# A first end output in a load buffer, and two of the last outputs stored in uneven partition pieces, in a rotation of an 8192x8192 matrix

## The chip, the cores and the metric

The kernel runs on one core of one Trainium2 chip. The time is the device time of that core in microseconds (us), as the median of several executions; the profiled execution is one more look, with its own span.

## The reference

```
x: 8192 x 8192 float32, k = 1
out = np.rot90(x, 1)          # out[r, c] = x[c, 8191 - r]
```

Each of 268 MB is read once and written once; nothing is computed.

## The kernel before

The matrix goes through the core in blocks of up to 1024 rows by 4096 columns. A block is loaded 128 rows at a time (2 MB per load, SyncE queue), VectorE reverses the columns within each block of 128 into small `ar` tiles, PE transposes 128x128 blocks into PSUM, ScalarE copies 128x2048 results to an `o` tile and issues its store on its own queue (2 MB per store). The last block is cut in two of 512 rows, called here the last two tiles; each has four outputs of 2 MB, `i` = 0 to 3, and the very last one is stored in two halves by columns. There are three `o` buffers and two `a` (load) buffers; at the end, when loads have run out, some outputs go to `a` buffers.

```python
def store(r0, rt, c0, chunks, end):
    ...
    for i, g0 in enumerate(range(0, W // P, G)):       # G = 8 blocks of 128 columns here
        if end and i % 2:
            ot = a_pool.tile([P, F], dt, tag="a")       # 2 buffers
        else:
            ot = o_pool.tile([P, F], dt, tag="o")       # 3 buffers
        o = ot[:, : G * rows].rearrange("m (g f) -> m g f", g=G)
        ...                                             # PE transposes into ps
            nc.scalar.copy(o[:, G - PW - h : G - h, :], ps[h // PW])
            done = h + PW
            if done % S == 0:
                dst = out[top : top + S * P, r0 : r0 + rows].rearrange("(g m) f -> m g f", g=S)
                nc.scalar.dma_start(out=dst, in_=o[:, G - done : G - done + S, :])
        yield
...
*_, chunks = load(*before_last)
outputs = store(*before_last, chunks, True)
rows = load(*last)
for _ in range(last[1] - 1):     # three of the four last loads
    next(rows)
next(outputs)                    # first end output
chunks = next(rows)              # the fourth load
```

## Time and profile before

| | before |
|---|---|
| time, median of 6 runs | 1267.64 us (1267.44 to 1268.09) |
| span of the profiled run | 1265.4 us |
| moved by DMA, over the span | 537.55 MB, 425 GB/s |
| busy share of PE, ScalarE, VectorE | 57%, 37%, 28% |

It is read by elimination: no compute engine is busy for more than 57% of the span, while the DMA engines are busy in all 40 slices. The lines for this, and what follows from them, stand in the prediction. One view that is used all through this text is not a view of the page: the completion records. A whole store adds to its semaphore 16 times in the trace, as many as the core has DMA engines (the page counts 4144 packets under 512 B, 16 for each of 128 loads and 131 stores); each increment is read here as one engine's, and sorted they show how many engines are early or late. They don't name the engine. The prediction's list times the small packets that write these increments; the increments themselves, used from here on, come some 0.4 us later (1264.32 and 1264.37 for its 1263.9 and 1264.0). In the views PE is TensorE and PEld its weight loads, DVE is VectorE, ACT is ScalarE, ACTq is ScalarE's instruction queue, where the issue of a DMA shows as the time that it holds the queue, and L167 is a line of the kernel.

### The profile page before, as it was taken

Reading aid. Unit: us, or ns where it says so; the run is one execution under the profiler, and the core shown is the slowest. Engines: PE = TensorE matmul, PEld = TensorE weight load, DVE = VectorE, ACT = ScalarE, POOL = GpSimd, SP = SyncE. Lnnn points to the kernel's source line nnn. Section 1 sums busy time; section 2 is a strip of 40 time slices with the busy share of each in tenths; the row PEclk is TensorE's granted clock in tenths of the full one; section 3 lists DMA queues with packets and bytes.
Section 4 is the critical chain, followed back from the end, with each engine's and each line's share of the span. In section 5 each row is a group of like instructions: output and inputs, shape, how many; then the busy total and the mean of one; then the engine's idle time right before and its main releaser. Section 6 shows DMA issues by size and latency. Waiting matters only on the chain.

```text
span 1265.4 us, 10391 instructions
## 1 busy us (share of the span) xinstructions
PE 721.2 (57%) x4096; PEld 680.0 (54%) x4096; DVE 355.2 (28%) x1024; ACT 466.6 (37%) x257; POOL 0.7 (0%) x6
## 2 busy tenths in 40 slices
PE   1554555566555565565655666556555566566573
PEld 1453555566545565555645655456555555555573
DVE  4423223322232222322233222322233222332210
ACT  0432433433334333343334333343333433343354
POOL 0000000000000000000000000000000000000000
PEclk9977777767777768777687776866867867767787
DMA  9999999999999999999999999999999999999998
GB/s 398 428 428 430 427 428 429 429 431 428 428 429 427 430 429 430 428 430 429 428 428 430 429 430 428 428 430 428 429 430 428 429 427 430 426 428 427 428 380 355
DMA packets 37345, 537.55 MB, mean 425 GB/s; under 512 B 4144, under 2 KB 4144, under 8 KB 4144
## 3 DMA queue, kind: packets, MB, share of 16 engines
q10 hardware_dynamic: 18864, 268.44, 50.0%
q1 hardware_dynamic: 18432, 268.44, 49.7%
q8 instruction: 32, 0.52, 0.2%
q14 instruction: 17, 0.14, 0.0%
HBM read 268.44 MB, written 268.44 MB: 424 GB/s over the span
## 4 chain that ended last, share of the span: by engine, by line
DMA 84%; ACT 13%; issue 1%; PE 0%; ACTq 0%; DVE 0%; SPq 0%
DMA out_dram<-ot 81%; ACT ot L167 13%; DMA a<-in_x_dram 3%; PE pt L146 0%; ACTq L175 0%; DVE ar L106 0%; ACTq L167 0%; SPq L101 0%
## 5 line engine op out<-in xcount | busy, mean ns | idle before, releaser
L146 PE MATMUL pt<-ident,ar 128*128 128x128 f32 x4096 | 721.2, 357 | 526.2 <-ACT ot L167 470.2
L146 PEld LDWEIGHTS pt<-ident,ar 128*128 128x128 f32 x4096 | 680.0, 191 | 567.2 <-ACT ot L167 505.0
L167 ACT COPY ot<-pt 128x2048 f32<-128x2048 f32 x256 | 465.3, 1870 | 757.5 <-DMA out_dram<-ot 719.6
L106 DVE COPY ar<-a 128x512 f32<-128x512 f32 x1024 | 355.2, 420 | 861.8 <-DMA a<-in_x_dram 705.7
L167 ACT ACT_TABLE_LOAD x1 | 1.3, 1283 | 25.6 <-DVE ar L106 25.6
masks.py:199 POOL TENSOR_SCALAR_AFFINE_SELECT ident<-ident 128x128 f32<-128x128 f32 x1 | 0.3, 292 | 0.1
masks.py:197 POOL MEMSET ident<- 128x128 f32 x1 | 0.2, 204 | 0.3 <-POOLq L215 0.3
L215 POOL MEMSET const-bfloat16-1.0<- 128x1 bf16 x1 | 0.1, 101 | 0.0
L215 POOL MEMSET const-uint8-127<- 128x1 uint8 x1 | 0.1, 101 | 0.0
L215 POOL MEMSET const-float32-0.0<- 128x1 f32 x1 | 0.1, 98 | 0.2 <-issue 0.2
L215 POOL MEMSET const-float32-1.0<- 128x1 f32 x1 | 0.1, 98 | 0.0
## 6 DMA issues: line engine op xcount, KB each, us to landing
a<-in_x_dram SPq DMA_DIRECT2D x128, 2048.0 KB, 16.6
out_dram<-ot ACTq DMA_DIRECT2D x125, 2048.0 KB, 25.7
out_dram<-ot ACTq DMA_DIRECT2D x6, 1024.0 KB, 26.8
```

The costliest lines, as they stand in the source:

```text
L106: nc.vector.tensor_copy(out=ar[:], in_=a[:, j * CH : (j + 1) * CH].rearrange("r (b m) -> r b m", m=P)[:, :, ::-1],)
L146: nc.tensor.transpose(ps[w // PW][:, PW - 1 - w % PW, t * P : (t + 1) * P], chunks[t, g * P // CH][:, g % (CH // P), :], ident,)
L167: nc.scalar.copy(o[:, G - PW - h : G - h, :], ps[h // PW])
L215: nc = _bacc.Bacc("TRN2", target_bir_lowering=False, num_devices=1)
```

## The change

The intent has two parts. First, the first output of the end goes to a load buffer that is already free, instead of waiting for an `o` buffer whose store is still under way; for that the fourth load is issued ahead of it in program order. Second, DMA engines that finish early at the end shall get more of the last two megabyte stores and late ones less, by means of pieces whose partition count decides how many engines take part (in the trace of the changed kernel, 16, 7, 15, 16, 7, 7 and 2 increments for pieces of 64, 49, 15, 112, 7, 7 and 2 partitions).

```diff
+UNEVEN = {1: [64, 49, 15], 2: [112, 7, 7, 2]}
...
             nc.sync.dma_start(
                 out=a[:], in_=x[r0 + t * P : r0 + (t + 1) * P, c0 : c0 + W]
             )
+            yield chunks
...
-            if end and i % 2:
+            if end and i % 2 == 0:
                 ot = a_pool.tile([P, F], dt, tag="a")
...
-                    nc.scalar.dma_start(
-                        out=dst, in_=o[:, G - done : G - done + S, :]
-                    )
+                    near = end and r0 + rows == N          # the very last tile
+                    p = 0
+                    for n in UNEVEN.get(i, [P]) if near else [P]:
+                        nc.scalar.dma_start(
+                            out=dst[p : p + n],
+                            in_=o[p : p + n, G - done : G - done + S, :],
+                        )
+                        p += n
...
-    for _ in range(last[1] - 1):
+    for _ in range(2 * last[1] - 1):
         next(rows)
     next(outputs)
     chunks = next(rows)
```

## The prediction

> **What bounds the kernel now.** I read the page first: strip of 40 slices, DMA queues, chain. It is a transposing copy, 268 MB in and 268 MB out:
>
> ```profile
> DMA  9999999999999999999999999999999999999998
> GB/s 398 428 428 430 427 428 429 429 431 428 428 429 427 430 429 430 428 430 429 428 428 430 429 430 428 428 430 428 429 430 428 429 427 430 426 428 427 428 380 355
> ...
> DMA 84%; ACT 13%; issue 1%; PE 0%; ACTq 0%; DVE 0%; SPq 0%
> ...
> out_dram<-ot ACTq DMA_DIRECT2D x125, 2048.0 KB, 25.7
> ```
>
> All 16 DMA engines are busy from end to end at about 428 GB/s; 536.9 MB at that rate is 1254 us of the 1265.4 us span. The compute engines are half idle. Only the first slice and the last two (380 and 355 GB/s) fall short: (428-380)/428 + (428-355)/428 of a 31.6 us slice is 3.5 + 5.4 = 8.9 us. The change can only touch those 8.9 us, of which the completion after the last byte (about 1.4 us, below) cannot go. [...]
>
> Next, the table of short stretches over the tail (columns: length; busy of PE, PEld, DVE, ACT, POOL; clock; DMA share; GB/s):
>
> ```profile
> 1205.00:1210.00 5.00, 2.44 (x11) 2.25 (x12) 1.24 (x4) 3.63 (x2) 0.00 (x0) 0.63 0.95 401
> 1210.00:1215.00 5.00, 3.98 (x23) 3.74 (x21) 0.78 (x3) 0.20 (x1) 0.00 (x0) 0.69 0.99 419
> 1215.00:1220.00 5.00, 3.28 (x16) 3.28 (x17) 2.00 (x6) 3.43 (x2) 0.00 (x0) 0.66 0.54 229
> 1220.00:1225.00 5.00, 4.79 (x44) 4.51 (x43) 0.00 (x0) 4.07 (x3) 0.00 (x0) 1.00 0.89 374
> 1225.00:1230.00 5.00, 4.42 (x41) 4.13 (x39) 0.00 (x0) 4.31 (x3) 0.00 (x0) 1.00 1.00 413
> ...
> 1260.00:1266.00 6.00, 0.00 (x0) 0.00 (x0) 0.00 (x0) 0.00 (x0) 0.00 (x0) 0.50 0.12 48
> ```
>
> So there are two losses: a hole at 1215 to 1225, when the loads have run out and the next store is not issued yet, and a ragged end after 1260. The ScalarE timeline says why the hole is there:
>
> ```profile
> 1209.30 0.55 ACTq L175 DMA_DIRECT2D out_dram<-ot  x1
> 1214.80 3.63 ACT L167 COPY ot<-pt 128x2048 f32<-128x2048 f32 x2 [5.53 <-DMA out_dram<-ot]
> 1218.46 0.55 ACTq L175 DMA_DIRECT2D out_dram<-ot  x1
> 1220.26 3.64 ACT L167 COPY ot<-pt 128x2048 f32<-128x2048 f32 x2 [1.83 <-PE pt L146]
> 1223.93 0.55 ACTq L175 DMA_DIRECT2D out_dram<-ot  x1
> ```
>
> The copy at 1214.80, of the first end output, sat 5.53 us until an old store (issued at 1189.68) had left its o buffer; then its store left at 1218.46, the next at 1223.93, and from there one every 4.31 us, faster than the 5.0 us that 2 MB takes.
>
> Last, the trace's raw records: one completion increment per DMA engine and store. I sorted the 16 increments of each store. Engine numbers are not recorded.
>
> ```
> store issued 1209.30: 6 engines at 1215.4-1215.6, 8 at 1217.2-1218.9, 2 at 1223.7 and 1224.1
> last half store:     12 engines at 1260.0-1260.3, 1261.6, 1262.1, then 2 at 1263.9 and 1264.0
> ```
>
> This is the central reading. Two engines lag. The spread is 0.4 us at 10 us into the run, 4 us at 100, and 15 us between first and last by 1100. The two laggards have packets back to back through the hole and to the end (16 KB in 0.626 us each), so **their total of packets sets the end**, and filling the hole cannot help them. From 1226 they do 53 full packets where the others do 47: 6 x 0.626 = 3.8 us late. The two at 1261.6 and 1262.1 each took an instruction-fetch packet (16 KB, about 1 us) in between.
>
> [...]the last packet ends at 1263.96 and the span at 1265.4, so 1.4 us of tail. [...]the change makes small ones; queued behind others, I expect that to be harmless.
>
> **The change part by part.**
>
> 1. First end output in the load buffer (with the load's issue moved ahead of it in program order, and the even outputs instead of the odd ones in load buffers). That buffer's last reader is a VectorE group at 1203.46 + 2.77 = 1206.2, so the copy no longer waits for the store until 1214.72. It waits for PE instead: the 28th of its 32 transposes, the last into the first PSUM half, ends at 1213.54 in the trace. So the copy starts at 1213.55 instead of 1214.80, 1.25 us earlier, and the store leaves at 1217.2. PE can then start the second output at 1215.45; at the 0.21 us per transpose that it needs there, 16 of them take 3.4 us, so its copy starts at 1218.9 and its store goes at about 1222.6 instead of 1223.93, 1.3 us earlier; all later ones follow. The hole, 4.3 + 0.5 us on the fast engines, shrinks by about 1.3 us. On the laggards: zero. Alone, this part should be worth about 0.
>
> 2. The pieces. [...]in 16 KB packets per engine, against 8 and 8:
>
> ```
> piece     64  49  15 | 112  7  7  2 | sum (16 before)
> 0, 1       4   7   1 |   7  1  1  1 | 22  (+6)
> 2 to 6     4   7   1 |   7  1  1  0 | 21  (+5)
> 7 to 14    4   0   1 |   7  0  0  0 | 12  (-4)
> 15         4   0   0 |   7  0  0  0 | 11  (-5)
> ```
>
> [...]-4 x 0.626 = -2.5 us and -5 x 0.626 = -3.1 us, so they end at 1261.4 and 1260.8. Engines 0 to 6: 1260.0 to 1260.2, less the 1.3 us of part 1, plus 3.1 or 3.75 us: 1261.9 to 1262.6. One of them that is hit by an instruction fetch ends up to 1.5 us later, near 1264. Engines 8 to 14: 1260.1 - 1.3 - 2.5 = 1256.3, early. So the last packet is near 1262.5, and both parts are needed: with the pieces alone engines 0 to 6 would end at 1263.2 to 1263.9, all gained being lost again.
>
> 3. Issue cost. Five more DMA issues at 0.547 us are 2.7 us on ScalarE's queue. Moreover the two last issues took 2.11 and 2.45 us (the timeline shows the pair as 4.60), against 0.55 to 0.65 everywhere else; [...]some pieces may stall for 2 to 3 us. The path: ScalarE starts 1.3 us earlier, loses 2.7 to 5 us, so the final store is issued 1.4 to 3.7 us later, 1251.6 to 1254 instead of 1250.2. Engines 0 to 6 do not reach it before about 1259, the laggards later still. Hidden. Engines 8 to 14 may run dry once or twice, but they have 6 us to spare.
>
> Sum: last packet 1263.96 -> about 1262.5 (1261.4 to 1264), so -1.5 us, and I lean a little further, to -1.9, because piece sizes this odd look like fitted ones. 1267.57 - 1.9 = 1265.7.
>
> **The rivals.** (a) [...]one is among 0 to 6: that one gets 5 or 6 packets more, and the end is 3.1 to 3.8 us later, 1271. [...]one in ten. (b) Part 1 does not start the stores earlier, because PE, at a granted clock of 0.66 there, becomes the wait: then 0 to 6 end at 1263.2 to 1263.9 and the time is 1267, unchanged. Only 1.25 us lie between PE's half and the present start of the copy, so this is the serious one. (c) Small DMAs stall ScalarE's queue so long that the last store comes late to the engines 0 to 6: issue after about 1257 would be needed, 7 us later than now; unlikely. (d) All the hole is filled and the split balances perfectly: the mean of the 16 end times is 1260.8, less about 1 us of filled hole, but the laggard with -4 packets still ends at 1261.4, so 1267.57 - 2.5 = 1265.1 is about the floor, give or take fetches.
>
> **Range and chances.** Floor 1265.1, less one us for a different fall of the fetch packets, centre 1265.7, and (b) at 1267 with some spread of its own; hence 1264.0 to 1267.6. Ends beyond 2% would need 25 us, three times what the whole tail loses: 0.01 faster, 0.01 slower.
>
> **What would show it.** The first end copy should wait for PE, not for a store, and its store leave near 1217.2; the stretch 1215 to 1220 should move clearly more than 229 GB/s. The last increments should show seven engines together near 1262, two near 1261, and seven idle from about 1256, so GB/s in the last 6 us falls before it stops. Three sizes of store with 64, 49 and 15 partitions should give 16, 7 and 15 increments by DMA. Wrong would be: laggards still at 1264 or later, a store issue that blocks beyond 1257, or a hole just as deep.

The sum comes to a last packet at about 1262.5 instead of 1263.96, -1.5 us, and to -1.9 us with the lean. Its -2.5 and -3.1 us are those of the two late engines; that these are among the engines that the pieces relieve was an assumption, with one chance in ten given against it. The division was an assumption too, but the changed kernel shows its counts: 16, 7, 15, 16, 7, 7 and 2 increments for its seven pieces, 70 in all where two whole stores have 32, and its page counts 18902 packets on the store queue instead of 18864, 38 more. Where there are fewer than 16, one more increment comes at the moment of issue. Engine numbers are labels: 0 to k - 1 stand for the k engines of a store with k increments, as if each smaller set lay within the larger ones. No record names an engine.

## The result, and the profile after

The changed kernel took 1275.13 us (median of 6 runs, 1274.16 to 1277.37) against 1267.64 us. The ratio is 1.0062, 95% interval 1.0049 to 1.0075: slower by 0.6%, within the 2% that count as the same, and outside the predicted range.

The strip of 40 slices of the changed kernel (its span is 1273.4 us, a slice 31.8 us):

```profile
GB/s 401 426 426 430 427 428 428 429 431 430 427 429 427 430 429 429 429 428 428 430 429 430 428 428 428 429 428 430 429 428 427 428 430 428 426 429 428 426 411 222
```

Thirty-eight slices are as before. The last but one rose from 380 to 411, the hole was partly filled; the last fell from 355 to 222. So the loss is all in the last slice. The short stretches over it (columns as in the prediction: length; PE, PEld, DVE, ACT, POOL busy; clock; DMA share; GB/s):

```profile
1215.00:1220.00 5.00, 4.42 (x41) 4.14 (x40) 2.25 (x7) 4.33 (x3) 0.00 (x0) 1.00 0.86 360
...
1235.00:1240.00 5.00, 3.84 (x35) 3.56 (x34) 0.00 (x0) 3.64 (x2) 0.00 (x0) 1.00 1.00 419
1240.00:1245.00 5.00, 0.76 (x7) 0.53 (x5) 0.00 (x0) 0.00 (x0) 0.00 (x0) 0.97 1.11 374
1245.00:1250.00 5.00, 0.00 (x0) 0.00 (x0) 0.00 (x0) 0.02 (x1) 0.00 (x0) 0.50 0.67 174
1250.00:1255.00 5.00, 3.10 (x15) 3.10 (x16) 0.00 (x0) 3.62 (x2) 0.00 (x0) 0.51 0.51 134
1255.00:1260.00 5.00, 2.07 (x19) 1.83 (x17) 0.00 (x0) 0.00 (x0) 0.00 (x0) 1.00 0.98 311
1260.00:1265.00 5.00, 0.00 (x0) 0.00 (x0) 0.00 (x0) 3.63 (x2) 0.00 (x0) 0.68 0.57 202
1265.00:1270.00 5.00, 0.00 (x0) 0.00 (x0) 0.00 (x0) 0.00 (x0) 0.00 (x0) 0.50 0.84 338
```

The kernel before, in three of the same stretches:

```profile
1240.00:1245.00 5.00, 4.42 (x40) 4.15 (x39) 0.00 (x0) 4.33 (x3) 0.00 (x0) 1.00 1.01 416
...
1255.00:1260.00 5.00, 0.00 (x0) 0.00 (x0) 0.00 (x0) 0.00 (x0) 0.00 (x0) 0.50 1.00 416
1260.00:1265.00 5.00, 0.00 (x0) 0.00 (x0) 0.00 (x0) 0.00 (x0) 0.00 (x0) 0.50 0.14 57
```

The stretch 1215 to 1220 now moves 360 GB/s where it moved 229. In the stretch from 1240, in which the first engines come to the first piece (their shares of the store ahead of it landed from 1242.3 on), the rate breaks. Compare two columns there, the share and the rate: at 1235 to 1240 a share of 1.00 moves 419 GB/s; at 1240 to 1245 a share of 1.11 moves only 374, and at 1245 to 1250 a share of 0.67 moves 174, that is 260 per unit of share. Where the share holds and the rate falls, the packets themselves take longer. Beside this there is true idleness (0.51 at 1250 to 1255).

The ScalarE timeline of the changed kernel, first the first end output, then the three outputs of the pieces:

```profile
1212.13 3.64 ACT L171 COPY ot<-pt 128x2048 f32<-128x2048 f32 x2 [3.28 <-PE pt L150]
...
1215.80 0.55 ACTq L184 DMA_DIRECT2D out_dram<-ot  x1
...
1238.77 11.11 ACTq L184 DMA_DIRECT2D out_dram<-ot  x3
1249.98 3.64 ACT L171 COPY ot<-pt 128x2048 f32<-128x2048 f32 x2 [11.23 <-issue]
...
1253.65 6.93 ACTq L184 DMA_DIRECT2D out_dram<-ot  x4
1260.62 3.63 ACT L171 COPY ot<-pt 128x2048 f32<-128x2048 f32 x2 [7.00 <-issue]
```

The last two issues of the kernel before, for comparison:

```profile
1248.04 4.60 ACTq L175 DMA_DIRECT2D out_dram<-ot  x2
```

The first end copy waits for PE now, no longer for a store, and its store leaves at 1215.80 instead of 1218.46. But the three pieces of the second output hold the queue for 11.11 us (1.15, 3.30 and 6.60 us each) and the four of the third for 6.93 us, and ScalarE's next copies wait behind them. The final half store is issued at 1264.28 instead of 1250.19.

The packet records show the rest. From 1238 us on, the changed kernel's 16 KB store packets (394 of them) have a median of 0.626 us as before, but 83 take over 1.0 us and 15 over 2.0 us, in heaps near 1.2 to 1.3 and near 2.4. In the kernel before 1 of 446 takes over 1.0 us.

There are thus three suspects: **partitions** (packets take longer while a store covers only part of the 128 partitions), **load** (the late engines got more, not fewer, packets) and **issues** (seven DMAs in place of two stall ScalarE's queue). Part 1 and the order of outputs is a fourth.

### The profile page after: what moved, and what is told of

It is laid out like the page before. It is cut to its first block, busy times and chain, and to the rows that moved or that the text cites. A ratio compares the mean times of both kernels' runs of the same rounds, so it can differ in the third digit from the quotient of the medians.

```text
span 1273.4 us, 10398 instructions
## 1 busy us (share of the span) xinstructions
PE 727.5 (57%) x4096; PEld 686.0 (54%) x4096; DVE 355.3 (28%) x1024; ACT 466.7 (37%) x257; POOL 0.7 (0%) x6
## 3 DMA queue, kind: packets, MB, share of 16 engines
q10 hardware_dynamic: 18902, 268.44, 50.1%
## 4 chain that ended last, share of the span: by engine, by line
DMA 81%; DVE 10%; ACT 4%; ACTq 2%; issue 2%; PE 1%; DVEq 0%; SPq 0%
DMA a<-in_x_dram 65%; DMA out_dram<-ot 16%; DVE ar L110 10%; ACT ot L171 4%; ACTq L184 2%; PE pt L150 1%; DVEq L110 0%; SPq L104 0%; ACTq L171 0%
```

## The experiments

Numbers that follow a cut in `even_split`, `contig16` and `stride16` are what was expected if the partitions are to blame; in `free_split` that suspect and the load gave the same numbers.

### One part at a time

`order_only` is the changed kernel without pieces; `pieces_only` is the kernel before with them.

```diff
-UNEVEN = {1: [64, 49, 15], 2: [112, 7, 7, 2]}
+UNEVEN = {}                                      # order_only
```

> The changed kernel with whole 128-partition stores at the end (the piece lists emptied), so part 1 alone. Every theory: the two laggards never idle, so 1267.2 to 1267.8 us, ratio to before 1.000 within 0.0005, although the stretch 1215 to 1220 moves about 360 GB/s instead of 229. If part 1 itself were the harm it would be above 1269.

> The kernel before with the piece lists alone. All theories that blame the pieces: 1273 to 1278 us, as slow as the full change or up to 2 us slower, as the hole at 1215 to 1220 stays as well. If order and pieces only harm together: near 1268.

`order_only` took 1267.27 us against 1267.53 us (ratio 0.9998, 0.9984 to 1.0013), `pieces_only` 1277.76 us (1.0077, 1.0060 to 1.0094). So the pieces do all of the harm, and part 1 alone is worth nothing, though it does what it was made for. Its stretches:

```profile
1215.00:1220.00 5.00, 4.42 (x41) 4.14 (x39) 2.77 (x8) 4.33 (x3) 0.00 (x0) 1.00 0.87 367
...
1255.00:1260.00 5.00, 0.00 (x0) 0.00 (x0) 0.00 (x0) 0.00 (x0) 0.00 (x0) 0.50 0.60 247
1260.00:1265.00 5.00, 0.00 (x0) 0.00 (x0) 0.00 (x0) 0.00 (x0) 0.00 (x0) 0.50 0.09 38
```

The hole is filled to 367 GB/s, and bytes are missing in turn at 1255 to 1260 (247 GB/s against 416 before). The completion records say why: fourteen engines end at 1257.2 to 1259.6 now, but the two late ones at 1264.1 and 1264.5, where they ended before (1264.3 and 1264.4). Time that is won by engines that do not set the end is given back as idleness at the end.

### The same load per engine, other partitions; and the same number of issues, all partitions

`even_split` takes pieces that go over all 16 engines evenly, so each engine moves 8 packets per output as in the kernel before (its four pieces have 64 increments, 16 each: the store queue has 18896 packets, 32 more than before, where two whole stores have 32). `free_split` issues as many DMAs as the change but cuts by column groups, so each covers all 128 partitions.

```diff
-UNEVEN = {1: [64, 49, 15], 2: [112, 7, 7, 2]}
+UNEVEN = {1: [64, 64], 2: [112, 16]}             # even_split
---
+UNEVEN = {1: [4, 3, 1], 2: [5, 1, 1, 1]}         # free_split, of the 8 column groups
-                            out=dst[p : p + n],
-                            in_=o[p : p + n, G - done : G - done + S, :],
+                            out=dst[:, g : g + n],
+                            in_=o[:, G - done + g : G - done + g + n, :],
```

> The changed kernel with the pieces 64, 64 and 112, 16: every piece goes over 16 engines, so each engine moves 8 packets per output as before. [...]packets of the 64s take about 1.25 us instead of 0.63, those of the 16 about 2.5 us, and the time is 1270 to 1274. Load theory (only the laggards' 5 or 6 extra packets count): packets of 0.63 us and 1267.5. Issue theory (each further DMA on the ScalarE queue stalls it): two issues more, about 1269.

> The changed kernel with as many issues as the change has, but the stores are cut by column groups of all 128 partitions (4, 3, 1 and 5, 1, 1, 1 of 8 groups)[...]. [...]load theory: 1267.2 to 1268 us, packets shorter but in proportion to their bytes. Issue theory: 1273 to 1276, with blocked issues of 3 to 6 us as in the change.

`even_split` took 1274.93 us (1.0058, 1.0043 to 1.0073), just above the band expected and as slow as the full change with no engine loaded more than another; `free_split` took 1266.80 us (0.9995, 0.9981 to 1.0010), as fast as the kernel before. The stretches of `even_split`:

```profile
1240.00:1245.00 5.00, 1.50 (x10) 1.26 (x9) 0.00 (x0) 2.91 (x2) 0.00 (x0) 0.78 1.03 364
1245.00:1250.00 5.00, 5.00 (x27) 5.00 (x26) 0.00 (x0) 0.73 (x1) 0.00 (x0) 0.54 1.07 236
1250.00:1255.00 5.00, 0.45 (x5) 0.21 (x2) 0.00 (x0) 0.22 (x1) 0.00 (x0) 0.81 0.88 220
1255.00:1260.00 5.00, 0.00 (x0) 0.00 (x0) 0.00 (x0) 3.42 (x2) 0.00 (x0) 0.50 0.82 244
```

At 1245 to 1250 the engines have no idle time at all (share 1.07) and move 236 GB/s, 56% of the 419 that a full share moves. Of its 408 packets of 16 KB after 1238 us, 111 take over 1.0 us. In `free_split` 1 of 154 does.

`free_split` also acquits the issues. Its timeline:

```profile
1236.76 7.52 ACTq L184 DMA_DIRECT2D out_dram<-ot  x3
1244.38 3.63 ACT L171 COPY ot<-pt 128x2048 f32<-128x2048 f32 x2 [5.88 <-issue]
1246.27 3.97 ACTq L184 DMA_DIRECT2D out_dram<-ot  x4
```

The queue was held for 7.52 us here too, and ScalarE waited for 5.88 us, with no effect on the end: the late engines still had enough to do. Whether the longer hold of the change (11.11 us), which leaves early engines idle, adds anything of its own was not tried apart from the slow packets; but the two late engines, which set the end, are not among the idle ones: their last increments (1267.55, then 1272.56 for both half stores, issued at 1262.52 and 1264.28) are 5.01 us apart, which is what eight packets of 0.626 us take, so they didn't wait for an issue there.

### Partitions, measured by themselves

`contig16` stores the second and third of the last outputs in 8 pieces of 16 neighbouring partitions each, `stride16` in 8 pieces of every eighth partition. Both issue as often, and I take it that both load the engines alike, with one partition per engine and piece: an estimate from `even_split`, where the piece of 16 partitions had 16 increments.

```diff
+                    for n in range(8 if near else 0):
+                        nc.scalar.dma_start(
+                            out=dst[n * 16 : (n + 1) * 16],                     # contig16
+                            in_=o[n * 16 : (n + 1) * 16, G - done : G - done + S, :],
+                        )
---
+                            out=dst[n : P : 8],                                 # stride16
+                            in_=o[n : P : 8, G - done : G - done + S, :],
```

> Part 1 alone, but the second and third of the last outputs are each stored in 8 pieces of 16 neighbouring partitions; every engine moves one partition per piece, so the load per engine is even. [...]packets take up to 2.5 us and the two outputs up to 40 us instead of 10: 1280 to 1297. A theory in which any small piece costs its issue: the same time as stride16.

> As contig16 in number and size of pieces, but each takes every eighth partition[...]. [...]packets of about 1.25 us, the two outputs up to 20 us instead of 10: 1272 to 1278, clearly below contig16. Issue theory: equal to contig16.

The packets differ:

```
16 KB store packets after 1238 us, by duration (us)
            under 0.9   0.9-1.5   1.5-2.0   over 2.0   all
contig16       222         81        60         42      405
stride16       213        201         7          1      422
before         443          3         0          0      446
```

`stride16` has its slow heap at 1.2 to 1.3 us (99 packets), twice 0.626, and hardly anything beyond; of `contig16` 42 take over 2.0 us, most of them below 2.6, about four times 0.626. The times follow in that order: 1279.95 us (1.0099) and 1277.34 us (1.0078); `contig16` is just below the band expected. So the way in which pieces of 16 are laid over the partitions changes the time of a packet. Whether that is the side of SBUF, where they are read, or the rows written in HBM is not shown: the two kernels also write their rows in another order, and no run kept the two apart.

### Load, measured by itself

`load7` and `load2` leave the stores whole and add five small stores of the same tile into a spare buffer, of 7 partitions or of 2, taking every fourth partition.

```diff
+                    if near and i in (1, 2):
+                        for e in range(3 if i == 1 else 2):
+                            nc.scalar.dma_start(
+                                out=spare[e if i == 1 else 3 + e],
+                                in_=o[e : e + 4 * 7 : 4, :, :],     # 4 * 2 in load2
+                            )
```

> Part 1 alone plus five extra stores of 7 partitions (0, 4, ... 24 and so on[...]) into a spare buffer: five 16 KB packets more for engines 0 to 6[...]. If both laggards are among 0 to 6, as the late increments of the change's 7-engine pieces suggest, the end moves by 5 x 0.626 = 3.1 us: 1270.4. [...]Packets stay at 0.63 us either way.

> The same with 2 partitions instead of 7: five packets more for engines 0 and 1 alone. If neither laggard is 0 or 1 (the change's 2-partition piece landed early): 1267.3, as part 1 alone. If one is: 1270.4.

Had neither late engine been among the seven, `load7` was expected at 1267.3 us. `load7` took 1270.51 us against 1267.20 us (1.0026, 1.0011 to 1.0041), `load2` 1267.55 us (1.0002, 0.9987 to 1.0017). All packets but one stayed under 0.9 us in `load7`. So five packets more on each of seven engines cost what five packets take, 3.1 us expected and 3.3 measured, which they only do if a late engine is among those seven. Each of the five small stores has two late increments (in the fourth 1262.2 and 1262.8, the other five engines by 1258.5), so both are. On the two engines of `load2` the packets cost nothing that can be measured. The number of engines is seen here as well: a piece of 7 partitions has seven increments, and one earlier one at the moment of issue.

`probe` adds such stores of 6, 5, 4 and 3 partitions; if the late ones were outside all of these engines, none of the four was to show a late increment.

> Part 1 alone plus four extra stores into a spare buffer[...]. Which of them show a late increment, some 5 us behind the others, tells which engines the laggards are: both should show in the store of 6 or 7 engines and none in that of 2; if the second laggard is engine 6, the store of 6 shows one only. Time about 1269 to 1270.[...]

One look, state unknown, 1269.0 us. The increments after the one made at issue:

```
6 engines: 1247.9 1248.0 1248.0 1249.4 | 1255.0 1255.2
5 engines: 1248.6 1248.6 1248.6        | 1255.7 1255.7
4 engines: 1249.2 1249.2 1249.2        | 1256.3
3 engines: 1249.8 1249.9 1249.9
```

Both late ones are among the five engines of one store, one among the four, none among the three. That fits sets of which each lies within the next larger one; which engines they are by number is not shown. In the changed kernel they are among the seven but not among the two: both late increments are there in its pieces on 7 engines (1260.2 and 1260.4 in that of 49 partitions), and its piece on 2 engines landed without one (1263.2 and 1264.0, before the late pair of the piece ahead of it, 1267.0 and 1267.6). That the pair is the same in every run is not shown; the runs come from several chips (the record names 12 for the first four, 4 for `load7` and `load2`, 11 for `probe`).

### Where the lag comes from, and a candidate

Two runs asked why two engines lag. Both give VectorE another number of instructions, since 8 KB instruction-fetch packets come in a rhythm of about 118 us that fits its 1361 instructions (they start at 36.8, 155.2, 273.4, 391.4 and 509.4 us and so on in the trace before; 1361 x 118 / 1265 is 127 instructions to a packet), and several of them seemed to fall on a late engine, a reading of packet records that no view shows. `wide_copies` halves the copies and would also be a faster kernel if the guess were right; `more_fetch` adds a small memset after each copy.

```diff
-CH = 512                                         # wide_copies
+CH = 1024
-    r_pool = ctx.enter_context(tc.tile_pool(name="r_pool", bufs=63))
+    r_pool = ctx.enter_context(tc.tile_pool(name="r_pool", bufs=31))
---
                 chunks[t, j] = ar                 # more_fetch
+                nc.vector.memset(spot[:], 0.0)
```

> Part 1 alone, with VectorE copies of 128x1024 instead of 128x512 (512 instead of 1024 of them, in 31 tiles instead of 63). A test of where the laggards' lag comes from, and a candidate. If it comes from the 8 KB instruction-fetch packets[...], some 11 of 17 of which fall in VectorE's rhythm of 118 us: 5 fewer such packets, the laggards about 2 to 5 us less late, 1263 to 1266. If the lag has another source: 1267.3, or later if the coarser tiles stall the loads.

> Part 1 alone plus 1024 VectorE memsets of one column, one after each copy, off the path. If the laggards lag because the 8 KB instruction-fetch packets of VectorE fall on them (about 1 us each, every 128 instructions), there are 8 more of them and the end moves by 4 to 9 us: 1271 to 1276, with the last increments later still behind the rest. If the lag has another source: 1267.3.

Neither decides it. `wide_copies` took 1291.49 us (1.0190, 1.0176 to 1.0204) and `more_fetch` 1283.55 us (1.0127, 1.0110 to 1.0144), both because of holes in the middle of the run, as their strips show (`wide_copies` first):

```profile
GB/s 398 426 426 429 429 429 409 430 393 411 429 386 430 417 405 429 410 430 410 411 426 395 428 423 413 429 387 429 427 408 428 408 429 423 407 427 411 428 427 377
```

```profile
GB/s 399 387 431 418 412 425 307 423 428 397 429 428 430 429 427 431 429 430 429 429 428 429 429 429 429 429 429 429 430 427 430 427 430 425 429 428 427 428 424 327
```

In the first, every second or third slice loses, perhaps because 31 wide tiles let the loads run ahead less than 63 narrow ones; in the second, several of the first ten slices lose, the seventh most. A hole lets late engines catch up (in the kernel before, the last increment came 8.7 us after the first for the store issued at 1209.30, and 4.5 us for the one issued at 1218.46, in the hole), so the lag at the end can't be compared. The fetch packets did change, from 17 to 12 and to 24. The guess was weak from the start: the expectation of `more_fetch` counts about 1 us for each 8 KB packet, but in the trace before they take 0.31 us, and it is the 16 KB fetch packets that take 0.94 to 1.03 us. The source of the lag stays open.

No version beat both kernels: `order_only` and `free_split` equal the kernel before within their intervals.

## Why the prediction was wrong

**What bounds the kernel** held. The DMA engines set the time, and within the tail the two late engines set the end: `order_only` fills the hole and gains nothing, and an extra load on other engines (`load2`) costs nothing.

**Part 1** held. The first end copy waits for PE, as foreseen. Its store left at 1215.80 instead of the 1217.2 worked out: PE began those 32 transposes 0.4 us earlier and took 5.40 us instead of 6.42, at a granted clock of 0.94 in 1210 to 1215 instead of 0.69. In `free_split`, where they took 6.43 us, it left at 1216.96, near the number worked out. The hole shrank by more than the 1.3 us worked out: the first engines end 3.2 us earlier in `order_only` (1257.2 instead of 1260.4). Its value of "about 0" was right. Rival (b) did not come about.

**The count of engines per piece** held: 16, 7, 15 and 2 increments where they were forecast.

**The step that failed first is that the two late engines would be among those that the pieces relieve** (-2.5 and -3.1 us in the prediction). No trace showed it, and rival (a) was given one chance in ten. The late engines are among the seven of the 7-engine pieces and not among the two of the last, so the pieces gave them 5 packets more instead of 4 or 5 fewer: plus 3.1 us instead of minus 2.5, as `load7` measured by itself. That alone would have made the time that rival (a) named, 1271.

**The second is the 0.626 us for each of those packets**, which was carried over from stores of 128 partitions, and the sentence on small pieces, "queued behind others, I expect that to be harmless". With pieces of 64, 64, 112 and 16 partitions 111 of 408 packets took over 1.0 us (`even_split`), with pieces of 16 neighbouring ones 42 of 405 over 2.0 us (`contig16`); the prediction has no term for this. What this cost is to be read from the last increment of each store, taken as one engine's (packets of 0.626 us; excess over them in brackets):

```
                       before             the change                     even_split
last tile, i = 0       1244.42-1249.42    1244.81-1252.43  (+2.6)        1244.13-1253.81  (+4.7)
i = 1                  -1254.41           64: -1254.94                   64: -1256.30
                                          49: -1260.35     (+1.0)        64: -1259.35     (+0.5)
                                          15: -1260.98
i = 2                  -1259.38           112: -1265.77    (+0.4)        112: -1265.42    (+1.7)
                                          7: -1266.40                    16: -1266.63     (+0.6)
                                          7: -1267.55      (+0.5)
i = 3, two halves      -1264.37           -1272.56                       -1271.64
```

In the change the excess is 2.6 + 1.0 + 0.4 + 0.5 = 4.5 us, and five packets more are 3.1 us; with the 0.4 us by which that engine was later at the outset it makes 8.0 of the 8.2 us between the ends. Its largest part is not in a piece at all: the late engine was still on a whole store, `i` = 0, which took 7.6 us instead of 5.0 (9.7 in `even_split`), while the engines ahead of it were already on the 64-partition piece. So I read it as the early ones slowing the late one; that is a reading of the slow packets and was not shown by itself. How much this way of balancing could give is not shown either: no run moved work off a late engine with nothing else changed.

**The issue cost and rival (c)** were mis-sized: stalls of "2 to 3 us" were 3.3 and 6.6 us, and the last store was issued at 1264.28, beyond the 1257 named as the limit. Yet the stall looks like a consequence more than a cause: with `free_split` the same number of issues stalls 7.5 us without harm, and the late engines didn't wait for the late issue. What makes the queue hold is not shown: an issue held it for 0.55 us as a rule, 2.1 and 2.5 us for the last two before, 6.6 us in the change, and two of them 8.93 us in `even_split`.

**The range** was built on a floor and on "no gain" as its upper end. The 3.1 us of rival (a) and the slow packets both lay above it; at one in ten, (a) alone did not move its edge. The centre was moved by a further 0.4 us because the piece sizes look fitted, for which there was no measurement.

## What to carry to other kernels

If a store like this must be cut, cut it by columns (`free_split`, no loss) and not by partitions (`even_split`, 7.4 us): there 111 of 408 packets took over 1.0 us, against 1 of 446 in the kernel before, and the late engine, still on an earlier whole store, took 9.7 us for it instead of 5.0. Before work is moved between DMA engines, find out by their increments in small probes which engines are late; in a DMA-bound kernel, filling a hole in which the late ones were never idle moves the idle time and not the end (`order_only`, ratio 0.9998).
